# An encoder layer on one core: a wider V projection, column tiles for memory attention, and new homes in on-chip memory

## The chip, the cores and the metric

The kernel runs on one core of a Trainium2 chip. Its time is device microseconds from the start of the program to its end. A core has five engines that run their own instruction streams in order and wait for each other by semaphores: TensorE (PE in the profile, with its weight loads as PEld), VectorE (DVE), ScalarE (ACT), GpSimd (POOL) and SyncE (SP), which here issues most of the transfers. Matrix products read both operands from SBUF (the on-chip memory, 128 partitions) and accumulate in PSUM, eight banks of 2 KB a partition.

## What is computed

One layer of a streaming encoder, all in float32, for 2048 new positions of one prompt and 8 streams ("sample") of 16 positions each. Cut to what matters here:

```python
def encoder_layer(x, past_k, past_v, ..., mk, mv, ...):
    h = rmsnorm(x, g_mix_pre)
    y, new_k, new_v, new_conv = parallel_mixer(h, ...)
    x = x + rmsnorm(y, g_mix_post)
    h = rmsnorm(x, g_mem_pre)
    x = x + rmsnorm(memory_attention(h, mk, mv, w_mq, w_mo), g_mem_post)
    h = rmsnorm(x, g_ffn_pre)
    f = (jax.nn.silu(h @ w_gate) * (h @ w_up)) @ w_down
    return x + rmsnorm(f, g_ffn_post), ...

def memory_attention(h, mk, mv, w_mq, w_mo):          # 4 heads of 256, 256 memory tokens
    q = (h @ w_mq).reshape(B, T, MEM_HEADS, MEM_HEAD_DIM)
    s = jnp.einsum("bthd,bmhd->bhtm", q, mk) * (MEM_HEAD_DIM ** -0.5)
    p = jax.nn.softmax(s, axis=-1)
    o = jnp.einsum("bhtm,bmhd->bthd", p, mv).reshape(B, T, D_MODEL)
    return o @ w_mo
```

The mixer projects h (1024 wide) to q, k, v (512 each) and to the value and gate of a gated unit. Attention has 8 heads of 64 over the own chunk of 64 positions and the 8 chunks before it, with a bias for each head that depends on the clipped distance of query and key. The gated unit goes through a causal convolution of width 31, a layer norm and a swish. Attention and convolution results side by side go through one output projection. The sample streams have memory keys and values of their own, given as input.

## The kernel before, in words

Activations are cut into 17 token tiles of 128 rows: 16 of the prompt and one, `S_TILE`, that holds the 8 sample streams of 16 rows. Nearly every product is made in three passes (`mm3`, L287; `mm3h`, L293): both operands are split into a rounded part "h" (type float32r) and the remainder "l", and high x high, high x low and low x high are summed. So each operand needs a copy on ScalarE (the rounded part) and a subtraction on VectorE or GpSimd (the remainder); for weights both are in `wload` (L275: transfer, L282 copy, L284 subtraction).

The order of stages is memory keys and values of the prompt (`phase_mem`), projections (`phase_proj`), attention, output projection (`mixout`), cross attention of the prompt (`phase_cross`), then the feed-forward stages `gate_up` and `down`. The program is written in one order; a planner with a simulated timeline then sets each engine's instruction order, and may draw an instruction forward when its operands and its place in memory are free. Places are chosen by hand: `Region.lay` and `Region.at` give each name a home in KB of a partition in the areas `sbF`, `sbR`, `fa`, `fb` and the flexible ones, with so many buffers in turn. Two names may share a home, and then the later one waits until the earlier one has been read.

*Projections.* Three groups of two subs of up to three token tiles. In a group come the gated unit (four column blocks j, value and gate), V, then k and q. The convolutions run in the background: each matmul block calls `tick`, which moves `conv_vector` (VectorE, L522) and `conv_pool` (ScalarE L531, GpSimd L532) on. V is made in two column halves `cg` (L630): each loads two blocks of weights, and for each token tile makes 24 products x 2 halves = 48 matmuls of 256 columns. The weight slots "wh" and "wl" have four buffers each, PSUM tile "mm" four. `bias_tables` (L251) spreads the reversed table of the bias over 128 rows in DRAM, [8, 128, 640], early on; attention reads one head of it at a time (L820, L880).

*Attention* (L732) walks through 128 units (head, token tile) and writes its result to `attT` (L873), 32 KB a partition at the start of `sbF`, ordered by head pair, then position. In the background run the sample streams' own attention (`sample`, L756), whose products use column tiles (`tile_position`, L775), and the last convolution norms (`late_norms`). `selectors`, `weigh` and `out_weights` make ready what the output projection needs.

*Output projection* (`mixout`, L963). Order: `S_TILE`, then 0 to 15. `prep` (L980) divides the attention result by the softmax sums: four matmuls of 128 columns (L989) spread the 16 rows of reciprocals (8 heads, rounded part and remainder) over 128 partitions, VectorE multiplies (L991), and the result is split (L997, L998). A token tile then has 48 matmuls of 512 columns (L297). At four points in it `ahead` is moved on, and from the third token tile so is a filler: `due += RATE` at each point, and as many filler steps as are due.

*The filler* is `cross_sample` (L1048), the memory attention of the sample tile. Its steps: query projection (8 steps of 6 matmuls), then 16 jobs (8 streams x 2 halves) for scores, softmax, 16 jobs for values, output projection (8 steps). A job loads 512 KB of memory keys or values (L1070), splits them (L1064, L1065) and makes eight matmuls of 256 columns (L1155, L1192). So that a stream's 16 queries meet only its own keys, they are put in a zeroed tile of 128 columns (`pad`, `blank`, `places` on GpSimd), in two places, and `gather` adds the two halves of the PSUM rows that belong together. Between stages `transposed` turns 128 x 128 blocks (L1080). What is left of the filler after the last token tile runs then.

*Cross attention* (`phase_cross`, L1207) of 16 token tiles begins with `norm(0)` (L1235: load, norm, L324 transposes, split to "sh"/"sl"), eight operands `f1` (L1226: load, L1231 copy, L1232 subtraction) and `scores`.

## Time and profile before

| | us |
|---|---|
| median of 3 runs | 2936.83 (2933.97 to 2940.01) |
| profiled execution, its time | 2935.2 |
| profiled execution, its span | 2933.3 |
| projections, all groups | about 107 to 612 |
| attention | about 612 to 869 |
| output projection with the filler | about 843 to 1119 |
| cross attention | about 1113 to 1515 |

The span is what lies between the first and the last instruction of the program. Stages overlap, so their edges are those of the first and the last matmul of each. In a row of the timeline the first number is the start in microseconds from the span's start, the second the length; "x8" is a run of eight like instructions shown as one, and a bracket gives the engine's idle time before it and what ended it. A group row ends with its count, busy time, mean length in ns and idle time before.

### The profile page before, as it was taken

What the parts mean: (1) busy time and instruction counts of PE and PEld (TensorE: products, weight loads), DVE (VectorE), ACT (ScalarE), POOL (GpSimd) and SP (SyncE); (2) the same over time, 40 slices, a digit from 0 to 9 for tenths busy, and PEclk for the clock granted to TensorE, in tenths of its full rate; (3) what the DMA queues carried; (4) which work ended last, traced back from release to release, by engine and by line L of the source; (5) the groups of instructions that cost most, each with busy time, mean ns of one, the idle gap of its engine ahead of it and who ended that gap; (6) DMA issues with size and microseconds to landing.
All of it is one profiled execution on the core that took longest, in us unless ns stands there. A gap on an engine that the chain in (4) does not pass through costs nothing.

```text
span 2933.3 us, 45550 instructions
## 1 busy us (share of the span) xinstructions
PE 2880.1 (98%) x16688; PEld 2638.1 (90%) x16688; DVE 2130.4 (73%) x3082; ACT 1338.5 (46%) x2631; POOL 1416.6 (48%) x1334
## 2 busy tenths in 40 slices
PE   9999999999999999999999999999999999999998
PEld 8999999988878887888879999999999999888786
DVE  7687895889985666344559888788888997555656
ACT  4435365678873444232344333433344444333433
POOL 1268495731123443154557565465556775424413
PEclk9999999999999999999999999999999999999999
DMA  8645253666635664232354333544344436656664
GB/s 290 245 130 190 94 162 112 218 220 212 224 115 171 220 220 154 69 129 96 129 201 172 116 134 115 200 159 155 141 140 152 145 142 228 224 171 226 225 217 147
DMA packets 201458, 499.53 MB, mean 170 GB/s; under 512 B 19801, under 2 KB 91361, under 8 KB 192394
## 3 DMA queue, kind: packets, MB, share of 16 engines
q1 hardware_dynamic: 186306, 427.01, 43.3%
q0 software_dynamic: 14928, 69.61, 6.4%
q8 instruction: 131, 2.15, 0.3%
q14 instruction: 93, 0.76, 0.1%
HBM read 365.45 MB, written 141.81 MB: 173 GB/s over the span
## 4 chain that ended last, share of the span: by engine, by line
PE 41%; DMA 4%; DVE 3%; POOL 2%; issue 1%; ACT 0%; DVEq 0%; POOLq 0%; SPq 0%; ACTq 0%
PE psb L291 13%; PE psb L290 13%; PE psb L289 13%; DMA sbf<-in_w_down_dram 2%; PE psb L297 1%; POOL sbf L1519 1%; DMA sbf<-x 1%; PE psb L1374 1%; DMA sbf<-hn 1%; DVE sbr L1589 0%; DVE sbr L1397 0%; DMA sbf<-in_w_gate_dram 0%; POOL sbf L347 0%; DVE sbx L1397 0%; DVE sbr L1523 0%
## 5 line engine op out<-in xcount | busy, mean ns | idle before, releaser
L289 PE MATMUL psb<-sbr 128*128 128x384 f32 (+3 forms) x2808 | 940.8, 336 | 4.8 <-DVE sbx L656 1.7
L290 PE MATMUL psb<-sbr 128*128 128x384 f32 (+3 forms) x2356 | 804.2, 341 | 0.5 <-DVE sbr L339 0.3
L291 PE MATMUL psb<-sbr 128*128 128x512 f32 (+3 forms) x1848 | 633.8, 344 | 4.2 <-DVE sbr L1589 4.0
L289 PEld LDWEIGHTS psb<-sbr 128*128 128x128 f32 x2808 | 529.7, 189 | 35.3 <-ACT sbr L1588 2.2
L291 PE MATMUL psb<-sbr,sbx 128*128 128x384 f32 (+2 forms) x1484 | 475.3, 321 | 0.0
L290 PEld LDWEIGHTS psb<-sbr 128*128 128x128 f32 x2356 | 444.4, 189 | 27.5 <-DVE sbr L339 1.0
L291 PEld LDWEIGHTS psb<-sbr 128*128 128x128 f32 x1848 | 348.4, 189 | 34.9 <-DVE sbr L1589 7.8
L297 PE MATMUL psb<-sbr 128*128 128x512 f32 x1200 | 292.5, 394 | 2.6 <-ACT sbr L1267 1.1
L1397 DVE TENSOR_TENSOR sbr<-sbf,sbr 128x512 fp32r<-128x512 f32 x258 | 262.7, 1021 | 39.7 <-ACT sbr L1396 38.9
L1396 ACT CAST sbr<-sbf 128x512 fp32r<-128x512 f32 x258 | 159.3, 620 | 280.2 <-PE psb L290 229.1
L291 PEld LDWEIGHTS psb<-sbr,sbx 128*128 128x128 f32 x1484 | 279.7, 189 | 0.1
L522 DVE SCALAR_TENSOR_TENSOR psb<-sbf,psb 128x768 f32<-128x768 f32 (+1 forms) x290 | 264.3, 911 | 6.2
L297 PEld LDWEIGHTS psb<-sbr 128*128 128x128 f32 x1200 | 222.1, 189 | 49.3 <-ACT sbr L1267 1.3
L1589 DVE TENSOR_TENSOR sbr<-sbf,sbr 128x384 fp32r<-128x384 f32 (+2 forms) x242 | 166.4, 711 | 95.3 <-ACT sbr L1588 94.1
L284 POOL TENSOR_TENSOR sbx<-sbf,sbr 128x1024 fp32r<-128x1024 f32 (+1 forms) x62 | 154.1, 2488 | 81.3 <-ACT sbr L282 70.2
L1588 ACT CAST sbr<-sbf 128x384 fp32r<-128x384 f32 (+2 forms) x242 | 112.5, 483 | 170.5 <-PE psb L290 153.9
L1519 POOL TENSOR_TENSOR sbf<-sbf 128x512 f32<-128x512 f32 x77 | 106.4, 1385 | 168.1 <-DMA sbf<-in_w_down_dram 166.2
L532 POOL TENSOR_TENSOR flexb<-flexb,flexb 128x128 f32<-128x128 f32 (+1 forms) x180 | 168.6, 937 | 26.2 <-ACT flexb L531 17.3
L289 PE MATMUL psb<-sbr,sbx 128*128 128x384 f32 (+1 forms) x524 | 170.6, 327 | 2.3 <-ACT sbx L1396 1.6
L1396 ACT CAST sbx<-sbf 128x512 fp32r<-128x512 f32 x153 | 94.7, 620 | 162.7 <-PE psb L290 142.8
L1397 DVE TENSOR_TENSOR sbx<-sbf,sbx 128x512 fp32r<-128x512 f32 x153 | 153.6, 1005 | 16.1 <-ACT sbx L1396 15.8
L1391 POOL TENSOR_TENSOR sbf<-sbf 128x512 f32<-128x512 f32 x66 | 97.9, 1484 | 107.4 <-DVE sbr L1397 50.7
(335 smaller groups left out, 6080.0 us busy)
## 6 DMA issues: line engine op xcount, KB each, us to landing
af<-flexb SPq DMA_DIRECT2D x33, 1344.0 KB, 5.9
sbf<-in_w_down_dram SPq DMA_DIRECT2D x154, 256.0 KB, 3.8
sbf<-in_w_gate_dram SPq DMA_DIRECT2D x66, 512.0 KB, 3.4
sbf<-in_w_up_dram SPq DMA_DIRECT2D x66, 512.0 KB, 3.4
sbf<-af SPq DMA_DIRECT2D x85, 384.0 KB, 4.1
sbf<-x SPq DMA_DIRECT2D x49, 512.0 KB, 3.7
sbf<-in_w_in_dram SPq DMA_DIRECT2D x48, 512.0 KB, 4.0
sbr<-ks POOLq DMA_DIRECT2D x16, 1024.0 KB, 8.4
```

What stands on the lines that cost most here:

```text
L284: self.lo_engine.tensor_tensor(lo[:, c], wf[:, c], hi[:, c].bitcast(F32), ALU.subtract)
L289: nc.tensor.matmul(ps, lh, rh, start=start, stop=False, **kw)
L290: nc.tensor.matmul(ps, lh, rl, start=False, stop=False, **kw)
L291: nc.tensor.matmul(ps, ll, rh, start=False, stop=stop, **kw)
L297: nc.tensor.matmul(y[o], l, r[:, o * 512:(o + 1) * 512], start=start and x == 0, stop=stop and x == 2)
L522: nc.vector.scalar_tensor_tensor(acc if w < CW - 1 else o, src(w), cwt[:, j, w:w + 1], acc, ALU.mult, ALU.add)
L532: nc.gpsimd.tensor_tensor(o, o, v, ALU.add)
L1396: nc.scalar.copy(hs[j][:, :], src[j])
L1397: nc.vector.tensor_tensor(ls[j][:, :], src[j], hs[j][:, :].bitcast(F32), ALU.subtract)
L1519: nc.gpsimd.tensor_tensor(acc[:, :], acc[:, :], q[:, :], ALU.add if s > 0 else ALU.subtract)
L1588: nc.scalar.copy(ch[:, m], a[:, x, m])
L1589: nc.vector.tensor_tensor(cl[:, m], a[:, x, m], ch[:, m].bitcast(F32), ALU.subtract)
```

## The change

In the order of the program:

- The bias table comes as an input of shape [8, 128, 640]; `bias_tables` is gone.
- V: four weight blocks `w_v[kq]`, each with 512 columns for two of the eight row blocks. A token tile has 24 matmuls of 512 columns; the two column halves are then read from one PSUM tile, in the same copies and stores as before. `tick` is called twice for each token tile.
- Late norms' homes move from 8 to 22 KB of `sbF`.
- `attT` is [P, 16, 4, P]: position tile first, then head pair.
- The selector: `by_column` writes on GpSimd the reciprocals of each head pair to their own 128 columns of a zero-padded tile `rj`, and one matmul of 512 columns takes the place of four. `by_column` is called a quarter of a token tile ahead of `prep`, and `weigh` a quarter later than before.
- Memory attention of the sample tile: `heads` makes four matmuls of 32 columns for a job, one for each head, at column tiles 0, 32, 64 and 96, with unsplit float32 operands (queries and probabilities as `sT`, keys and values straight from their load). A PSUM tile then has 32 rows for each head (16 of the stream, 16 that are not used) and 256 columns for each stream, so the probabilities and the result have 16 blocks to transpose each in place of 8. The softmax is made for four streams at a time, its last product on GpSimd. Padding and gathering are gone.
- `RATE` is 1.3 in place of 1.0.
- `phase_cross`: other homes for "sh", "sl", the operands `f1` and part of `f2`.

```diff
-RATE = 1.0
+RATE = 1.3
...
-                   .lay(sbF, 8, ("thx", 2, 1), ("zx", 2, 2), ("xnx", 2, 2))
+                   .lay(sbF, 22, ("thx", 2, 1), ("zx", 2, 2), ("xnx", 2, 2))
...
-            for cg in range(2):
-                wv = [self.wload(A["w_v"][cg, kh]) for kh in range(2)]
...
+            wv = [self.wload(A["w_v"][kq]) for kq in range(4)]
+            for hsub, sub in zip(hs, subs):
+                hh, hl, _, _ = hsub
+                for i, t in enumerate(sub):
+                    ps = self.t(ps_mm, [P, 512], F32, "mm")
+                    tc_ = slice(i * P, (i + 1) * P)
+                    for k in range(KC):
+                        wh, wl = wv[k // 2]
+                        c = slice((k % 2) * 512, (k % 2 + 1) * 512)
+                        self.mm3(ps[:, :], hh[:, k, tc_], hl[:, k, tc_], wh[:, c], wl[:, c], k == 0, k == KC - 1)
+                    tick()
+                    tick()
...
-        toep = self.toep
+        toep = A["toep"]
...
+    def by_column(self, t):
+
+        R = 2 * H
+        rt = self.rts.pop(t)
+        self.nc.gpsimd.tensor_tensor(self.rj[:R], rt[:, :].bitcast(F32).unsqueeze(1).to_broadcast([R, 4, P]),
+                                     self.own[:, :].unsqueeze(2).to_broadcast([R, 4, P]), ALU.mult)
...
-                for j in range(4):
-                    nc.tensor.matmul(pt[:, j * P:(j + 1) * P], self.expand[:, j, :], rt[:, :], start=True, stop=True)
+                nc.tensor.matmul(pt[:, :], self.spread[:, :, :].rearrange("p o d -> p (o d)"),
+                                 self.rj[:, :, :].rearrange("p j q -> p (j q)"), start=True, stop=True)
...
             if 0 < i < len(order) - 1:
+                self.by_column(order[i + 1])
+                yield
                 prep(order[i + 1])
...
+        def heads(out, s, x, left, right):
+
+            for h_ in range(MH):
+                nc.tensor.matmul(out[32 * h_:32 * h_ + 32, s % 4, :], left(h_), right[:, h_ * NM:(h_ + 1) * NM],
+                                 start=s % 2 == 0 and x == 0, stop=x == 1, tile_position=(0, 32 * h_),
+                                 skip_group_check=True)
...
+        ahead = Ahead([lambda s=s, x=x: load(A["cache_mem_kT"][s, x]) for s, x in jobs])
         yield
+        for s, x in jobs:
+            kx = next(ahead)
+            if x == 0 and s % 4 == 0:
+                sc = self.t(ps_so, [P, 4, NM], F32, "so")
+            heads(sc, s, x, lambda h_: qT[:, 2 * h_ + x, s * DEC_S:(s + 2) * DEC_S], kx)
             yield
+            if x == 1 and s % 4 == 3:
+                g = slice(s - 3, s + 1)
+                nc.vector.tensor_reduce(nmx[:, g], sc[:, :, :], axis=AX.X, op=ALU.max, negate=True)
+                for v in range(s - 3, s + 1):
+                    nc.scalar.activation(z[:, v, :], sc[:, v % 4, :], AF.Exp, bias=nmx[:, v:v + 1],
+                                         accum_out=sm[:, v:v + 1])
+                nc.vector.reciprocal(ri[:, g], sm[:, g])
+                for v in range(s - 3, s + 1):
+                    nc.gpsimd.tensor_scalar(z[:, v, :], z[:, v, :], ri[:, v:v + 1], None, ALU.mult)
...
-                .at("sh", 4, (sbR, [44, 40, 24])).at("sl", 4, (sbR, [52, 48, 28]))
+                .at("sh", 4, (sbR, [96, 44, 24])).at("sl", 4, (sbR, [100, 52, 28]))
...
-        for k, o in enumerate((56, 64, 80, 0, 8, 16, 72, 88)):
+        for k, o in enumerate((64, 80, 88, 0, 8, 16, 72, 56)):
...
-        spots = [(sbR, o) for o in (32, 36, 96, 100, 104)] + [(fr, 4 * i) for i in range(11)]
+        spots = [(sbR, o) for o in (32, 36, 40, 48, 104)] + [(fr, 4 * i) for i in range(11)]
```

More of the change, by code (lines that the diff above doesn't have):

```diff
@@ L1198, in cross_sample @@
-        oT = []
-        yield from transposed(col(of), oT)
+        qT = self.t(pool, [P, KC, P + DEC_S], F32, "sT", 1)
+        nc.gpsimd.memset(qT[:, :, P:], 0.0)
+        for k0 in range(0, KC, 4):
+            nc.scalar.copy(qT[:, k0:k0 + 4, :P], turn(col(q), k0)[:, :, :])
+            yield
+        z = self.t(pool, [P, DEC_B, NM], F32, "sh", 1)
+        nmx, sm, ri = [self.t(pool, [P, DEC_B], F32, x, 1) for x in ("nmx", "sm", "ri")]
+        ahead = Ahead([lambda s=s, x=x: load(A["cache_mem_kT"][s, x]) for s, x in jobs])
@@ new lines, in cross_sample @@
+        yield
+        pT = self.t(pool, [P, 2 * DEC_B, P], F32, "sT", 1)
+        for k0 in range(0, 2 * DEC_B, 4):
+            nc.scalar.copy(pT[:, k0:k0 + 4, :], turn(by_pair(z), k0)[:, :, :])
+            yield
+        of = self.t(pool, [P, DEC_B, NM], F32, "sh", 1)
+        ahead = Ahead([lambda s=s, b=b: load(A["cache_mem_v"][s, b * P:(b + 1) * P, :]) for s, b in jobs])
+        yield
+        for s, b in jobs:
+            vx = next(ahead)
+            if b == 0 and s % 4 == 0:
+                o = self.t(ps_so, [P, 4, NM], F32, "so")
+            heads(o, s, b, lambda h_: pT[:, 2 * s + b, 32 * h_:32 * h_ + 32], vx)
+            if b == 1 and s % 2 == 1:
+                nc.scalar.copy(of[:, s - 1:s + 1, :], o[:, s % 4 - 1:s % 4 + 1, :])
+            yield
@@ L1200, in cross_sample, with token @@
+        def token(k):
+            s, x = k // 2, k % 2
+            return (lambda t: t[:, :, :].rearrange("p (h x) n -> p x h n", x=2)[:, x, :, s * DEC_S:(s + 1) * DEC_S],
+                    lambda pt: pt[:, k % 4, :].rearrange("p (h n) -> p h n", n=32)[:, :, :DEC_S])
+        oT = yield from turned(by_pair(of), [token(k) for k in range(2 * DEC_B)])
         gpost = self.gain(pool, "g_mem_post", "sgain")
@@ L1650, in layout @@
     wv = i["w_in"][0][:, 1024:1536]
[L1651 removed]
+    o["w_v"] = wv.reshape(4, 2, P, 512).transpose(0, 2, 1, 3).reshape(4, P, D)
     o["w_out"] = i["w_out"].reshape(KC, P, D)
```

227 lines of the change are left out of this document (67 added, 160 removed).

## The prediction

> **What bounds the kernel now.** I read the head of the page first, then the busy time by stage. The columns of the second fence are the stretch, its length, the busy time of TensorE, its weight loads, VectorE, ScalarE and GpSimd with their instruction counts, the granted clock, the DMA share and GB/s.
>
> ```profile
> span 2933.3 us, 45550 instructions
> ...
> PE 2880.1 (98%) x16688; PEld 2638.1 (90%) x16688; DVE 2130.4 (73%) x3082; ACT 1338.5 (46%) x2631; POOL 1416.6 (48%) x1334
> ```
>
> ```profile
> 52.00:118.00 66.00, 65.51 (x436) 60.68 (x436) 50.10 (x77) 33.33 (x46) 15.51 (x14) 1.00 0.89 312
> 359.30:394.10 34.80, 34.80 (x293) 34.80 (x292) 31.15 (x40) 21.10 (x31) 31.79 (x18) 1.00 0.46 140
> 913.00:992.00 79.00, 79.00 (x400) 65.13 (x399) 48.03 (x60) 32.34 (x55) 30.16 (x50) 1.00 0.60 205
> 1066.00:1112.00 46.00, 46.00 (x228) 38.61 (x228) 28.75 (x26) 21.05 (x36) 19.02 (x28) 1.00 0.67 237
> 1119.00:1150.00 31.00, 26.06 (x114) 20.89 (x112) 20.62 (x19) 13.01 (x23) 13.45 (x8) 0.94 0.57 190
> ```
>
> TensorE is busy for 98% of the span, and for all of the V stage of the second group (359 to 394 us), of the key part of the sample rows' memory attention (913 to 992) and of the stretch before the stage ends (1066 to 1112). So in these stages a microsecond of matmul taken out is a microsecond off the end, and work taken from VectorE or ScalarE alone is worth nothing. The exception is 1119 to 1150, the hand-over from the output projection to cross attention, where TensorE stands still for 5 of 31 us at a mean clock of 0.94.
>
> **The price of a matmul by its width.** Matmuls overlap, so I take distances between starts, not durations (columns: start, length, engine, line, operation, tiles, shape, count).
>
> ```profile
> 359.33 0.28 PE L289 MATMUL psb<-sbr 128*128 128x256 f32 x1
> ...
> 393.87 1.04 PE L336 MATMUL psb<-ident,sbf 128*128 128x128 f32 x8
> ```
>
> ```profile
> 979.69 5.87 PE L297 MATMUL psb<-sbr 128*128 128x512 f32 x25
> 985.40 1.11 PE L1155 MATMUL psb<-sbr,flexb 128*128 128x256 f32 x8
> 986.35 1.12 PE L1155 MATMUL psb<-flexb 128*128 128x256 f32 x8
> ...
> 990.44 0.66 PE L989 MATMUL psb<-sbr 16*128 16x128 f32 x4
> 991.03 0.39 PE L1155 MATMUL psb<-sbr,flexb 128*128 128x256 f32 x1
> ```
>
> Between the two rows of the first fence lie the 288 V matmuls of six token tiles (48 each): 34.54/288 = 0.120 us for 256 columns. In the second, 25 matmuls of 512 columns take 5.71 us, 0.228 each; a job of memory attention (eight of 256 columns) takes 0.95; the four selector matmuls of a token tile take 0.59.
>
> **V at 512 columns.** A token tile has 48 matmuls of 256 columns and gets 24 of 512: 48 x 0.120 - 24 x 0.228 = 0.29 us, and 17 tiles save 4.9. The copies and stores behind it stay the same instructions.
>
> Its price is the weight buffers. All four 1024-column blocks are now needed by every token tile, so they fill the four "wh"/"wl" slots; before, two were in use while the next two were made ready. A block needs a copy on ScalarE and a subtraction on GpSimd:
>
> ```profile
> 359.39 1.05 ACT L282 CAST sbr<-sbf 128x1024 fp32r<-128x1024 f32 x1 [2.72 <-POOL sbx L284]
> ...
> 360.52 2.41 POOL L284 TENSOR_TENSOR sbx<-sbf,sbr 128x1024 fp32r<-128x1024 f32 x1 [1.76 <-ACT sbr L282]
> ```
>
> ```profile
> 393.67 1.84 POOL L532 TENSOR_TENSOR flexb<-flexb,flexb 128x768 f32<-128x768 f32 x1
> 395.46 4.78 POOL L284 TENSOR_TENSOR sbx<-sbf,sbr 128x1024 fp32r<-128x1024 f32 x2
> ```
>
> From the start of the copy to the end of the subtraction is 3.5 us, and a convolution step of 1.84 us can lie ahead of it on GpSimd, which is busy for 31.8 of 34.8 us here. At the start of V the third block waits for the slot of the last gate block, and its first use comes 12 x 0.228 = 2.7 us later: late by 0.8 us, or 2.6 behind a convolution step. At the end, the first key block waits for the first V slot, which comes free 18 x 0.228 = 4.1 us before the last V matmul: late by 0 to 1.3. Other token tiles' first halves and the next group's transposes can fill such holes. Six edges, three groups with two each: I take 0.7 us an edge, 4 us in all; the bounds are 0 and 2 us an edge, 12.
>
> **The selector.** Four matmuls of 128 columns become one of 512 over zero-padded 128 rows: 0.59 - 0.23 = 0.36 us, over 16 tiles 5.8. In front of it stands a new GpSimd product of 512 columns. Its nearest row:
>
> ```profile
> L1391 POOL TENSOR_TENSOR sbf<-sbf 128x512 f32<-128x512 f32 x66 | 97.9, 1484 | 107.4 <-DVE sbr L1397 50.7 <-DVE sbx L1397 34.6 <-DVE flexb L1397 10.4
> ```
>
> 1.5 us on an engine that is busy for 30 of 79 us in 913 to 992; a quarter of a token tile (3.7 us, below) lies between its call and the matmul, and the selector's consumer is needed half a tile later still. Without that cover it costs 16 x 1.5 = 24 us; I take 0.
>
> **Memory attention in column tiles.** A job's eight full-array matmuls become four of 32 columns, one for each head, side by side, with unsplit f32 operands. The nearest row is the attention of the sample rows, which works so already with 272 columns (eight records: each of the four runs as two passes):
>
> ```profile
> 681.74 0.38 PE L854 MATMUL psb<-ident,flexb 128*128 128x128 f32 x2
> 682.05 0.67 PE L775 MATMUL psb<-sbf,flexb 128*32 128x272 f32 x8
> 682.65 0.39 PE L836 MATMUL psb<-sbr 128*128 128x256 f32 x1
> ```
>
> ```profile
> 1092.29 1.03 PE L1080 MATMUL psb<-ident,flexb 128*128 128x128 f32 x8
> ```
>
> The group takes 0.60 us to the next matmul. A transpose takes (1.03 - 0.27)/7 = 0.11 us, so after the two of the first row the group could have begun at 681.96; it began 0.09 us later. That makes 0.69, for 256 columns some 0.66, against 0.95: 32 jobs save 9.3 us. The bounds are 8.3 (0.69) and 15 (0.48, the streaming alone without the changes of form). The probabilities and the result now need 16 transposes each in place of 8: 16 x 0.11 = 1.8 us more. Net 7.5, bounds 6.5 and 13.
>
> [...]
>
> With the splits go 32 copies of 1.05 us on ScalarE, 32 subtractions on VectorE and all of the padding on GpSimd: nothing, since TensorE is full there. New waits: TensorE now waits for the transfer itself, and the softmax of four streams sits between two groups of jobs on one PSUM tile.
>
> ```profile
> 1141.02 1.23 DVE L1249 TENSOR_REDUCE sbf<-psb 128x4 f32<-128x1024 f32 x1 [5.40 <-PE psb L297]
> 1144.24 0.18 DVE L1256 RECIPROCAL sbf<-sbf 128x4 f32<-128x4 f32 x1 [2.00 <-ACT sbf L1253]
> ```
>
> That chain took 3.2 us in cross attention. A call comes every 3.7 us (a quarter of the 15.0 us token tile worked out below), with output-projection matmuls between; I take 0, bound 3, behind which those matmuls would queue.
>
> **Bias table, token-tile order, early homes.** The table was built at 186 us and first read at 530, so its removal is worth 0; the attention result in the other order costs the same instructions, 0.
>
> What these homes, and the quicker filler, change is the hand-over. The filler had 64 steps and 60 calls at one a call, so the last output-weight matmuls ran after the last token tile; now it has 68 steps and 60 x 1.3 = 78, and ends nearly two tiles early. Cross attention's first tiles no longer lie under the whole attention result, nor its first operands under the last output weights.
>
> ```profile
> 1112.92 1.03 PE L324 MATMUL psb<-ident,sbf 128*128 128x128 f32 x8
> ...
> 1114.77 1.21 PE L297 MATMUL psb<-sbr,sbx 128*128 128x512 f32 x4 [0.35 <-DVE sbr L1065]
> ...
> 1118.12 1.19 PE L297 MATMUL psb<-flexb,sbx 128*128 128x512 f32 x4 [0.74 <-DVE flexb L1065]
> ...
> 1122.56 1.93 PE L324 MATMUL psb<-ident,sbf 128*128 128x128 f32 x8 [3.25 <-DVE sbr L326]
> ...
> 1132.26 3.03 PE L297 MATMUL psb<-sbr 128*128 128x512 f32 x12 [0.59 <-POOL sbr L1232]
> ```
>
> The idle times are 0.35 + 0.74 + 3.25 + 0.59 = 4.9 us. After the longest, eight transposes took 1.93 us against 1.03: the clock had fallen, about 1.9 us with the matmuls behind them. Of 6.8 us I take 5; bounds 0 and 7. Late next is the first probabilities' copy at 1149 us, which no part touches.
>
> **The sum** against the profiled execution's 2935.2 us (span 2933.3, 1.9 around it): -4.9 + 4 - 5.8 - 7.5 - 5 = -19.2, so 2916 us. The runs shown have a median of 2936.8, 1.6 above the profiled one; I leave that inside the range. With all bounds at their best the sum is -32 (2903), at their worst -2 (2933).
>
> **Rivals.** *The weight slots eat it:* each edge of the V stage stands for 4 us (copy, subtraction and a convolution step in a row, nothing to fill); six edges cost 24 instead of 4: 2936, no change. For it: GpSimd is 91% busy there. Against: the holes have work to fill them, and a first half of a token tile is 2.7 us long.
>
> *The transfers bound the filler (slower):* a token tile takes 48 x 0.228 + 5.2 x 0.66 and 0.6 for the rest, 15.0 us, and moves 5.2 x 0.52 MB of cache and 1.3 MB of its own rows, 4.0 MB: 268 GB/s. If these queues gave only the 205 of 913 to 992, a tile would take 19.6 us, and the 32/5.2 = 6.2 tiles of the caches 29 us more: 2945. It decides below 4.0 MB/(15.0 + 19.2/6.2) = 221 GB/s. For it: TensorE now waits for the landing. Against: the same kind of transfer ran at 312 GB/s in 52 to 118, and the queue has landings of
>
> ```profile
> DMA to landing us min/median/max: 3.2/4.2/6.7
> ```
>
> against two calls, 7.4 us, of lead.
>
> *The hand-over stays:* the filler ends early but cross attention's loads are still late on VectorE, 2921; the change then does not do what its homes say. *Column tiles don't run side by side:* four in turn, 4 x 0.48, would add 32 x 0.97 = 31 us: 2947. The rows speak against it, eight records in 0.67 us.
>
> **How the numbers follow.** The forecast with its bounds has 0.67, the hand-over that stays 0.15, the weight slots 0.08, the transfers 0.06, column tiles in turn 0.04 (with any other slower order). Within 0.2% (6 us, about what a measurement here can tell from no change) lie most of the weight-slot case. Faster 0.85, same 0.06, slower 0.09. The range is 2901 to 2933: the bounds of the sum, with 2 us more below since the runs shown lie up to 3 us under their median.
>
> **What would show it.** Right: some 440 fewer TensorE records (V 408, selector 48, plus 16 transposes); L1155 and L1192's successors as groups of eight 32-column records, 0.6 us to the next; TensorE busy about 18 us less; no gap over 1 us before cross attention's first transposes and a clock of 1.00 there. Wrong: TensorE idle on GpSimd's weight subtraction at the V edges; TensorE waiting for DMA of the memory caches; a 3 us gap still at the hand-over.

## The result, and the profile after

The changed kernel takes 2933.84 us (median of 12 runs, 2930.3 to 2939.61) against 2937.35 for the kernel before on the same chips (12 runs): a ratio of 0.9988, with a 95% interval of 0.9978 to 0.9998. So 3.5 us are gained where 19.2 were forecast, and the time lies 0.8 us above the range. The profiled execution took 2939.42 us, near the upper end of its runs, so stages are compared below, not spans.

The lines of the changed kernel are shifted: the three-pass matmuls of the output projection are L279 (before L297), the selector L979 (L989), memory-attention jobs L1095 (L1155, L1192), their transposes L1057 (L1080), the post-norm of a token tile L1031 to L1037 (L1036 to L1042), that of the sample tile L328 to L330 (L346 to L348), cross attention's norm L303, split L307/L308 and transposes L306 (L321, L325/L326, L324), its operands L1188, L1191, L1192 (L1228, L1231, L1232), weight splits L264/L266 (L282/L284), the filler's weight splits L1075/L1076 (L1064/L1065).

The head of the page and the busy time by stage (stretch, length, busy time with instruction counts of TensorE, weight loads, VectorE, ScalarE and GpSimd, granted clock, DMA share, GB/s):

```profile
span 2937.6 us, 44541 instructions
...
PE 2873.1 (98%) x16248; PEld 2594.9 (88%) x16248; DVE 2072.0 (71%) x3053; ACT 1306.7 (44%) x2623; POOL 1413.3 (48%) x1298
```

```profile
913.00:992.00 79.00, 79.00 (x426) 55.46 (x425) 29.02 (x47) 21.39 (x57) 29.00 (x34) 1.00 0.67 234
992.00:1066.00 74.00, 74.00 (x400) 50.24 (x399) 27.84 (x55) 21.72 (x63) 30.21 (x36) 1.00 0.68 233
1066.00:1105.00 39.00, 39.00 (x177) 31.90 (x175) 20.05 (x18) 17.48 (x32) 17.72 (x18) 1.00 0.49 158
1105.00:1119.00 14.00, 6.73 (x19) 5.25 (x19) 7.29 (x6) 4.22 (x5) 11.39 (x10) 0.63 0.32 111
1119.00:1150.00 31.00, 29.31 (x141) 24.06 (x140) 16.70 (x21) 13.35 (x27) 7.94 (x7) 1.00 0.53 175
```

There are 16688 - 16248 = 440 fewer matmul records, as worked out. TensorE's busy time fell by 7.0 us, not 18; apart from the end of the program the changed kernel ran 30.7 us at half clock and the one before 10.2, which lengthens its matmuls (384 columns in 0.32 us at 551.50 us, in 0.18 at 549.04 at full clock) by up to (30.7 - 10.2)/2 = 10 us. TensorE is full through the filler (913 to 1105), with 233 GB/s and more while the caches come in (913 to 1066), so the transfers don't bound it. But from 1105 to 1119 it is busy for 6.7 of 14 us at a clock of 0.63. The timeline there, of all engines (start, length, engine, line, operation, tiles, idle time before and its releaser):

```profile
1095.79 0.63 POOL L1037 DMA_DIRECT2D x<-flexb  x1
...
1103.50 1.28 DVE L328 SCALAR_TENSOR_TENSOR flexb<-psb,flexb 128x1024 f32<-128x1024 f32 x1 [7.21 <-issue]
...
1104.86 3.25 POOL L329 TENSOR_TENSOR flexb<-flexb 128x1024 f32<-128x1024 f32 x1 [7.84 <-DVE flexb L328]
...
1108.44 0.63 POOL L330 DMA_DIRECT2D x<-flexb  x1
...
1111.51 1.41 DVE L1035 SCALAR_TENSOR_TENSOR flexb<-psb,flexb,sbf 128x512 f32<-128x512 f32 x2 [5.60 <-DMA x<-flexb]
...
1112.32 8.44 PE L279 MATMUL psb<-sbr 128*128 128x512 f32 x24 [7.27 <-DVE flexb L1035]
```

Read it from below. TensorE waits 7.27 us with the last column half of the last token tile, since its PSUM buffer is still to be read by the post-norm of the token tile before it (L1035). That post-norm waits 5.60 us for a store: the sample tile's post-norm (L328, add L329, store L330) has just written the one home "po", which both post-norms use with a single buffer, and the home is free only when its store has landed. The sample tile's post-norm had itself been held up by that home: the store of an earlier token tile (L1037, issued at 1095.79) landed at 1103.42, and L328 began at 1103.50, although the profile puts its 7.21 us of idling down to issue. In the kernel before the filler ended behind the last token tile (its post-norm at 1133.2 us, the last token tile's at 1112.8), so the two never met. From 1107.8 us the clock is at half for 10.24 us, of which the last 5.8 fall on matmuls: 7.3 + 5.8/2 = 10.2 us are lost here.

The end of the program is longer too. At its end each engine's stream has records called DRAIN, and the engines then wait for each other (the last DRAIN of all five begins between 2937.1 and 2937.3 us in the changed kernel). These are GpSimd's in the kernel before, and then GpSimd's and SyncE's in the changed one (count, shortest/median/longest in ns, first and last start in us):

```profile
L1702 POOLq DRAIN  x3: 93/188/1343, 2927.4 to 2932.8; - x3
```

```profile
L1663 POOLq DRAIN  x3: 40/102/9014, 2927.8 to 2937.3; - x3
L1663 SPq DRAIN  x3: 7/7/7, 2932.0 to 2937.1; - x3
```

GpSimd's longest takes 1.34 us before and 9.01 us after, where it ends at 2936.8 us while SyncE has come to its own at 2932.0. From the end of the last matmul to the end of the program there are 8.3 to 8.8 us in the kernel before and its three variants (e3, e6, e12 below), and 12.7 to 13.0 us in the changed kernel and its 15 variants: some 4 us that the forecast has no term for. V, the selector, memory attention, the pace and the shared home are not the cause, since each of them was changed back or moved in some variant without changing this. The bias table as an input, the order of the attention result and the other homes remain, and no run tells them apart.

Where the time of each profiled execution went, by the first matmul of attention's scores, of the output projection, and of the transposes of cross attention's first probabilities (us; ratios of all runs to the kernel before, with their 95% intervals):

| kernel | to attention | attention | output projection to probabilities | ratio of times |
|---|---|---|---|---|
| before | 611.9 | 230.7 | 304.3 | 1 |
| after | 608.7 | 232.7 | 301.9 | 0.9988 (0.9978 to 0.9998) |
| after, own home | 608.1 | 233.2 | 293.8 | 0.9953 (0.9941 to 0.9966) |
| own home, product on VectorE | 609.6 | 233.0 | 289.8 | 0.9936 (0.9924 to 0.9949) |
| own home, old selector | 607.9 | 230.9 | 294.1 | 0.9961 (0.9947 to 0.9974) |
| own home, old memory attention | 608.8 | 234.9 | 293.4 | 0.9951 (0.9937 to 0.9965) |
| the same, product on VectorE | 607.8 | 231.4 | 295.2 | 0.9960 (0.9946 to 0.9973) |
| after, V at 256 columns | 611.7 | 232.2 | 300.8 | 0.9991 (0.9982 to 1.0) |
| before, new selector | 613.5 | 231.0 | 297.6 | 0.9972 (0.9962 to 0.9981) |

The stages are those of one execution each. What follows them, to the last matmul, took between 1774 and 1785 us in these and the other executions, though no experiment edits it; so a stage's microsecond or two need not show in the time.

### The profile page after: what moved, and what is told of

It reads as the page before. It is cut to its first block, busy times and chain, and to the rows that moved or that the text cites. A ratio compares the mean times of both kernels' runs of the same rounds, so it can differ in the third digit from the quotient of the medians.

```text
span 2937.6 us, 44541 instructions
## 1 busy us (share of the span) xinstructions
PE 2873.1 (98%) x16248; PEld 2594.9 (88%) x16248; DVE 2072.0 (71%) x3053; ACT 1306.7 (44%) x2623; POOL 1413.3 (48%) x1298
## 4 chain that ended last, share of the span: by engine, by line
PE 41%; DMA 4%; POOL 3%; DVE 3%; issue 2%; ACT 0%; SPq 0%; DVEq 0%; POOLq 0%; ACTq 0%
PE psb L273 13%; PE psb L272 13%; PE psb L271 13%; DMA sbf<-in_w_down_dram 2%; PE psb L279 1%; POOL sbf L1479 1%; DMA sbf<-x 1%; PE psb L1334 1%; DMA sbf<-in_w_gate_dram 0%; DVE sbr L1549 0%; DMA sbf<-hn 0%; DVE sbr L1357 0%; POOL sbf L329 0%; DVE sbx L1357 0%; DMA hn<-sbf 0%
## 5 line engine op out<-in xcount | busy, mean ns | idle before, releaser
L271 PE MATMUL psb<-sbr 128*128 128x384 f32 (+3 forms) x2672 | 916.5, 345 | 4.5 <-ACT sbr L1548 1.7
L272 PE MATMUL psb<-sbr 128*128 128x384 f32 (+3 forms) x2356 | 805.2, 342 | 0.5 <-DVE sbr L321 0.3
L273 PE MATMUL psb<-sbr 128*128 128x512 f32 (+2 forms) x1712 | 610.2, 358 | 3.7 <-DVE sbr L1549 3.6
L271 PEld LDWEIGHTS psb<-sbr 128*128 128x128 f32 x2672 | 503.8, 189 | 40.0 <-ACT sbr L1548 3.5
L272 PEld LDWEIGHTS psb<-sbr 128*128 128x128 f32 x2356 | 445.3, 189 | 27.4 <-DVE sbr L321 1.0
L273 PEld LDWEIGHTS psb<-sbr 128*128 128x128 f32 x1712 | 322.0, 188 | 39.7 <-DVE sbr L1549 7.5
L273 PEld LDWEIGHTS psb<-sbr,sbx 128*128 128x128 f32 x1484 | 280.2, 189 | 1.9 <-POOL sbx L266 1.8
L1356 ACT CAST sbr<-sbf 128x512 fp32r<-128x512 f32 x258 | 159.1, 620 | 275.7 <-PE psb L272 232.2
L279 PE MATMUL psb<-sbr 128*128 128x512 f32 x984 | 244.2, 397 | 9.7 <-DVE flexb L1035 7.3
L279 PEld LDWEIGHTS psb<-sbr 128*128 128x128 f32 x984 | 184.0, 190 | 55.0 <-DVE flexb L1035 7.5
L266 POOL TENSOR_TENSOR sbx<-sbf,sbr 128x1024 fp32r<-128x1024 f32 (+1 forms) x62 | 151.1, 2440 | 80.4 <-ACT sbr L264 70.5
L279 PE MATMUL psb<-sbr,sbx 128*128 128x512 f32 x750 | 186.7, 396 | 2.7 <-DVE sbx L989 1.8
L1479 POOL TENSOR_TENSOR sbf<-sbf 128x512 f32<-128x512 f32 x77 | 107.0, 1393 | 169.8 <-DMA sbf<-in_w_down_dram 168.1
L279 PEld LDWEIGHTS psb<-sbr,sbx 128*128 128x128 f32 x750 | 139.6, 189 | 37.1 <-issue 3.3
```

The costliest lines, as they stand in the source:

```text
L266: self.lo_engine.tensor_tensor(lo[:, c], wf[:, c], hi[:, c].bitcast(F32), ALU.subtract)
L271: nc.tensor.matmul(ps, lh, rh, start=start, stop=False, **kw)
L272: nc.tensor.matmul(ps, lh, rl, start=False, stop=False, **kw)
L273: nc.tensor.matmul(ps, ll, rh, start=False, stop=stop, **kw)
L279: nc.tensor.matmul(y[o], l, r[:, o * 512:(o + 1) * 512], start=start and x == 0, stop=stop and x == 2)
L1356: nc.scalar.copy(hs[j][:, :], src[j])
```

## The experiments

Each kernel's ratio is to the kernel before on the same chip. Many kernels have five runs, and their intervals reach about 0.0013 (4 us) to either side.

### The shared home, and the filler's pace

"Own home" gives the sample tile's post-norm the place of the queries and probabilities, which are read out by then; e1 instead lets the filler run to the end of the stage again.

```diff
-RATE = 1.3
+RATE = 1.15                                    # e1 alone
...
-    def postnorm(self, pool, y, xt, gbc, dst, dma=None, bufs=2):
+    def postnorm(self, pool, y, xt, gbc, dst, dma=None, bufs=2, tag="po"):
-        o = self.t(pool, [P, D], F32, "po", bufs)
+        o = self.t(pool, [P, D], F32, tag, bufs)
...
-                .lay(ft, 0, ("sT", 8, 1))
+                .lay(ft, 0, ("sT", 8, 1)).at("pos", 4, (ft, [0]))
...
+        self.postnorm(pool, flat(y), xt, gpost, self.x2[S_TILE], bufs=1, tag="pos")
```

> The changed kernel, rate 1.3, with a home of its own for the sample tile's post-norm output in place of the single one that it shares with the output projection's token tiles. Theory A1 (the shared home is the longer part of the gap: the next token tile's post-norm waited 5.6 us for the sample tile's store): the gap at 1105 us falls from 7.3 to 3 to 4.5 us, what ScalarE, GpSimd and VectorE need for one post-norm, and the time falls by 3 to 5 us. Theory A2 (the missing cover alone): a gap over 6 us stays, time within 2 us of the changed kernel.

> The changed kernel with a filler rate of 1.15 in place of 1.3: 60 calls give 69 steps, so the 68 filler steps last to the end of the last token tile. Theory A (the 7.27 us gap at 1105 us of the changed kernel stands because the filler is used up two token tiles early, so nothing covers the wait of a token tile's second PSUM half for the post-norm of the one before): no TensorE gap over 2.5 us between 1050 and 1125 us, no half-clock window there, and a time 6 to 10 us under the changed kernel's, about 2926. Theory B (the gap comes from cross attention's first loads, drawn forward into the in-order streams of ScalarE, VectorE and GpSimd): the gap stays within 2 us of 7.3, time within 3 us of the changed kernel.

The own home gave 2927.49 us, 0.9953. Its timeline at the same place:

```profile
1097.69 1.28 DVE L328 SCALAR_TENSOR_TENSOR flexb<-psb,flexb 128x1024 f32<-128x1024 f32 x1 [0.76 <-POOL flexb L289]
...
1101.75 0.60 POOL L330 DMA_DIRECT2D x<-flexb  x1 [0.30 <-POOL flexb L329]
...
1105.23 1.41 DVE L1035 SCALAR_TENSOR_TENSOR flexb<-psb,flexb,sbf 128x512 f32<-128x512 f32 x2 [1.00 <-POOL flexb L289]
...
1106.04 5.32 PEld L279 LDWEIGHTS psb<-sbr 128*128 128x128 f32 x24 [0.26 <-DVE flexb L1035]
1106.04 5.74 PE L279 MATMUL psb<-sbr 128*128 128x512 f32 x24
```

The sample tile's post-norm still stands between two token tiles, but L1035 no longer waits for its store, and TensorE's weight loads wait 0.26 us and its matmuls for nothing the row shows, in place of 7.27. No half-clock stretch follows, the stage is 8.1 us shorter, and the time some 10 us. That is more than theory A1 expected (a gap of 3 to 4.5 us left, 3 to 5 us gained): L328 begins at 1097.69 and no longer at 1103.50, so the home had cost twice. The home is the cause of the gap.

The slower filler of e1 gave nothing (2940.4 us, 0.9999, interval 0.999 to 1.0008), since another wait takes the place:

```profile
1111.65 1.04 ACT L1191 CAST sbr<-sbf 128x1024 fp32r<-128x1024 f32 x1 [7.02 <-DMA sbf<-f1s]
...
1115.85 1.01 ACT L307 CAST sbx<-psb 128x1024 fp32r<-128x1024 f32 x1
...
1116.91 1.22 PE L279 MATMUL psb<-sbr,sbx 128*128 128x512 f32 x2 [6.15 <-ACT sbx L307]
```

ScalarE waits 7.02 us for a weight of cross attention, and the split of cross attention's first token tile (L307) is queued behind it on the same engine. So the filler must neither end late nor write into the shared home. Three runs asked whether the pace alone matters, two of them with the home free.

> The own-home kernel with the filler at 1.2 steps a call in place of 1.3, the control for the run with the old memory attention. If only the shared home was the matter: 0.9953 as with 1.3. If a filler that ends later delays cross attention's first operands, as at 1.15: idle times of 1 us and more appear between 1100 and 1130 us, and the time is 0.997 to 0.999.

> The kernel before with nothing changed but the filler rate, 1.3 in place of 1.0: its 64 steps are used up after 49 of 60 calls, nearly three token tiles early. Theory A: the same kind of gap opens in the last three token tiles (one or more of 3 to 7 us, waiting for the post-norm's VectorE instruction), and the time is 5 to 12 us above the kernel before. Theory B (early homes and early loads make the gap, not the rate): no such gap, and the time is at or below the kernel before, by up to 5 us, since the filler no longer runs past the last token tile.

> The kernel before with the filler at 1.3 steps a call (which alone gave 1.002) and the sample tile's post-norm in another home than the token tiles'. Theory A1 (the shared home is what a filler pays that ends between two token tiles, in either kernel): faster than 1.002 by the gap before the next token tile's matmuls, 1.5 us, and the half clock that follows: about 1.001. Theory B (the old kernel loses to the faster filler because cross attention's first operands and first tiles are late there, under the output weights and the attention result): no change, 1.002 within 0.0005, with the idle times of 2.7, 1.8 and 2.6 us behind the last token tile still there. Neither expects it below 0.9985: a faster filler with a free home is not by itself the gain.

With the own home, 1.2 in place of 1.3 gave 2933.37 us, 0.9978 (0.9969 to 0.9987), 7 us slower; so the home was not the only matter. The wait is that of e1:

```profile
1102.87 0.32 SPq L1164 DMA_DIRECT2D flexb<-x  x1
...
1103.28 3.91 SPq L1188 DMA_DIRECT2D sbf<-f1s  x2
...
1108.45 1.04 ACT L1191 CAST sbr<-sbf 128x1024 fp32r<-128x1024 f32 x1 [3.28 <-DMA sbf<-f1s]
...
1111.95 1.01 ACT L307 CAST sbx<-psb 128x1024 fp32r<-128x1024 f32 x1
...
1113.01 1.22 PE L279 MATMUL psb<-sbr,sbx 128*128 128x512 f32 x2 [5.78 <-ACT sbx L307]
```

On SyncE's queue (SPq) these weight loads stand behind the filler's last load (L1164, the sample tile's own rows), which the slower filler issues at 1102.87; at 1.3 it went out at 1095.27. The kernel before at 1.3 steps a call is slower than at 1.0: 1.002 (1.0011 to 1.0029), and 1.003 (1.0021 to 1.004) with an own home, still with 2.7 us of waiting for ScalarE's L1231 behind the last token tile. There the shared home (moved to another place than in the own-home kernel) is not what costs; the quicker filler pays only together with the other parts.

### V

e4 puts V back to two halves of 256 columns; e5 is the own home with the late subtraction moved.

```diff
+                    self.lo_engine = nc.vector if last and which == 1 and j == 0 else nc.gpsimd     # e5
                     blk = self.wload(A["w_in"][which * 4 + j])
```

> The changed kernel with V as it was, in two column halves of 256. If V at 512 columns is worth what its matmul distances say (4.9 us) less the waits seen at its edges (1.6 us idle at 550 us and a half-clock window of 3.4 us behind it, some 3.3 us in all): the first attention matmul comes 1.5 us later than in the changed kernel, the gap at 550 us is gone, and the time is 0 to 3 us higher. If the weight slots cost more than the matmuls save: the first attention matmul comes earlier and the time is lower by 1 to 4 us.

> The kernel after with the sample tile's post-norm in a home of its own, and besides: in the third group the weight subtraction of the first key block after V is made on VectorE in place of GpSimd. Theory C (the late subtraction at the end of V is a real loss): the idle 1.6 us before the first key matmul at 550 us goes, and with it the half-clock stretch of 3.4 us (1.7 us of work); 3.3 us less than the kernel with the own home alone, about 0.994 of the time before against 0.9953. Rival (the wait is for the weight slot that the last V matmuls hold, whichever engine subtracts): the idle time stays within 0.4 us of 1.6 and the time stays at 0.9953.

In the table V at 512 columns brings attention forward from 611.7 to 608.7 us; in time it is lost in the scatter (0.9991 against 0.9988). Over all executions with nothing changed at the edge, attention began between 607.2 and 609.6 us with V at 512 (12 kernels) and between 611.7 and 614.0 with V at 256 (5 kernels); the means differ by 4.5 us. Four of these five also build the bias table; the fifth, e4, began 3.4 us behind the mean of the 12. Attention then took 232.7 us in the mean of the 12, against 231.1 in the kernel before and its variants, but V is not what costs there: e4, with V at 256, took 232.2, and e8, with V at 512 and the old selector, 230.9. What does is open. One edge of the six shows, the end of V in the last group, where no next group's work fills the hole:

```profile
549.34 0.28 PE L272 MATMUL psb<-sbr 128*128 128x256 f32 x1
551.21 0.49 PE L273 MATMUL psb<-sbr,sbx 128*128 128x384 f32 x1 [1.59 <-POOL sbx L266]
551.50 0.52 PE L271 MATMUL psb<-sbr 128*128 128x384 f32 x1
```

With the subtraction on VectorE the wait fell to 1.12 us, which neither theory had, and the time did not move: 0.9953 (0.9939 to 0.9967). Attention began 1.7 us earlier than in the own-home kernel (606.4 against 608.1), and with the product on VectorE 0.8 us earlier (e15 against e11, 608.8 against 609.6). So the edge is real, and its repair worth too little for these runs to tell in the time.

### The selector

e8 is the own home with the four matmuls of before and no product; e12 the kernel before with the new selector alone; e11 the own home with the product on VectorE.

```diff
-        self.nc.gpsimd.tensor_tensor(self.rj[:R], ...
+        self.nc.vector.tensor_tensor(self.rj[:R], ...          # e11
```

> The own-home kernel with the selector of the kernel before: four matmuls of 128 columns over 16 rows, no product on GpSimd. Theory E (the trace's price: the selector's share of start-to-start time was 9.4 us in the kernel before and 5.0 after): 3.9 to 4.4 us slower than the own-home kernel, 0.9967 of the time before. Prediction's price 5.8 us: 0.9973. Rival E2 (the wait for the product on GpSimd ahead of the matmul eats what the matmuls save): 0.9953, no change.

> The kernel before with the new selector alone (one matmul of 512 columns over 128 padded rows, the product on GpSimd ahead of it). The prediction's price: 5.8 us less, 0.998. Theory E (matmul starts say 4.4 us less): 0.9985. Theory E2 (start-up of the selector at attention's start and the first token tiles' products at the start of the output projection give it back as idle time and half clock): 1.000 within 0.001, with a half-clock stretch near 612 or 872 us that the kernel before has not.

> The own-home kernel with the selector's product on VectorE in place of GpSimd. Theory G (the product on GpSimd holds up VectorE: its 8-element cast took 1.01 us beside the product and 0.17 without it, and so the second token tile's split is late by 0.9 us at 872): the short casts beside it are back at 0.2 us, the idle time at 870 us falls from 1.76 to about 0.9, the half-clock stretch of 871 goes (3.4 us of work), and the time is 3 us under the own-home kernel, 0.9943. Rival G2 (VectorE's own 0.5 us for the product costs the same): 0.9953, the idle time stays over 1.5 us.

Alone in the kernel before, the selector gave 0.9972 (8.2 us; 6.7 in its stage), so the forecast's 5.8 was about right, and the theory that it is given back (E2) fell, though a half-clock stretch of the kind that it named is there, 3.41 us at 875.65. Taken out of the own-home kernel it cost nothing that can be told (0.9961 against 0.9953; 0.3 us in the stage). That kernel, e8, has none of the own home's two half-clock stretches, 6.83 us each at 612 and 872 us; at most 3.4 us of work each, they can hide the selector's gain. For the second the product explains a part. With it on GpSimd (own home), at the start of the output projection:

```profile
870.31 1.34 POOL L939 TENSOR_TENSOR sbr<-sbr,sbf 16x512 fp32r<-16x512 f32 x1 [3.91 <-ACT sbr L933]
...
870.67 1.01 DVE L926 CAST sbr<-sbf 128x8 fp32r<-128x8 f32 x1
...
871.60 1.28 DVE L989 TENSOR_TENSOR sbx<-flexb,sbx 128x512 fp32r<-128x512 f32 x2
...
872.33 2.08 PE L279 MATMUL psb<-sbr,sbx 128*128 128x512 f32 x4 [1.76 <-DVE sbx L989]
```

and with it on VectorE:

```profile
867.00 0.68 DVE L939 TENSOR_TENSOR sbr<-sbr,sbf 16x512 fp32r<-16x512 f32 x1
...
872.67 0.17 DVE L926 CAST sbr<-sbf 128x8 fp32r<-128x8 f32 x1
872.75 1.29 DVE L989 TENSOR_TENSOR sbx<-flexb,sbx 128x512 fp32r<-128x512 f32 x2
...
873.49 2.93 PE L279 MATMUL psb<-sbr,sbx 128*128 128x512 f32 x6 [0.86 <-DVE sbx L989]
```

A cast of eight columns took 1.01 us beside the product and 0.17 without it, and TensorE's wait for the split of the first token tile behind it (L989) fell from 1.76 to 0.86 us. The half-clock stretch there fell from 6.83 to 3.41 us, the stage from 293.8 to 289.8, and the time to 2919.48 us, 0.9936. The interval overlaps that of the own-home kernel (0.9924 to 0.9949, 0.9941 to 0.9966); a second pair with the same difference, e5 and e15, gives 292.5 and 289.1 us in the stage, 0.9953 and 0.9943. So the gain is likely, and a few microseconds at most. Nor is the product needed for such a wait: the kernel before, which has none, waits 1.74 us there (L998), without a half-clock stretch. The long cast ended with the product, both at 871.7 us; what ties the two is not shown.

### Column tiles

e7 issues each job's matmuls twice (so scores and values come out doubled); e10 issues the two jobs of a stream together, 36 steps at 0.7 a call; e13 has the memory attention of before at 1.2 steps a call, and e16 (1.2) and e17 (1.3) the same with the product on VectorE.

```diff
+            for r in range(2):                                                         # e7
             for h_ in range(MH):
                 nc.tensor.matmul(out[32 * h_:32 * h_ + 32, s % 4, :], ...
...
-            yield                                                                      # e10
+            if x == 1:
+                yield
```

> The own-home kernel with the matmuls of each memory-attention job issued twice (the scores and the values come out doubled). It measures what a job of column tiles costs when no change of tiling lies between. Theory D (a job costs 0.57 us of streaming and what it takes to change form once for each call, 0.09 us): 32 x 0.57 = 18 us more than the own-home kernel, 0.9953 + 0.0062 = 1.0015 of the time before. Rival D2 (two passes of 0.24 us are all that streams, the rest is the change of form): 32 x 0.48 = 15.4 us, 1.0005. Rival D3 (the jobs lie in holes of TensorE): under 5 us, below 0.997.

> The own-home kernel with the sample rows' memory attention of the kernel before (eight full-array matmuls a job, split operands, padding on GpSimd; its key caches in the old layout), the filler at 1.2 a call for its 64 steps so that it ends at about the same call. It prices the column tiles as a whole. Prediction's term: 7.5 us slower than the own-home kernel, 0.9979 of the time before. Theory H (start-to-start sums: jobs 31.4 against 25.1 us, transposes 3.1 against 5.3): 4.1 us slower, 0.9967. Rival H2 (what the column tiles save is given back by TensorE waiting, so undoing them costs nothing): 0.9953.

> The own-home kernel with the selector's product on VectorE and the memory attention of the kernel before, the filler at 1.2 a call. Beside the run with column tiles and the product on VectorE (0.9936, and 0.9943 with the edge) it prices the column tiles where the start of the output projection is quiet. Prediction's term: 7.5 us slower, 0.9962 to 0.9968. Sums of matmul starts: 4 us slower, 0.995 to 0.9957. Rival H2 (worth nothing): 0.994.

> The same at 1.3 a call, the pace of the kernel after. If the pace decides only by where the filler ends (64 steps at 1.2 end at the same call as 68 at 1.3; at 1.3 they end a call or two sooner): within 0.0005 of the run at 1.2. If the meeting of single instructions at the hand-over decides: 0.002 or more apart, with an idle time of 3 us and more between 1100 and 1130 us in one of the two.

> The own-home kernel with the two memory-attention jobs of a stream issued together (36 steps at 0.7 a call), nothing else. Theory F: groups of 16 records of 1.00 us instead of groups of 8 of 0.57, 3.6 us less between the first output matmul and cross attention's first probabilities (290.2 in place of 293.8 us), 0.994 of the time before. Rival F2 (transfers): idle times on DMA of the caches, no better than 0.9953.

TensorE's rows of the changed kernel, and then of e7 (32, 16 records in a run):

```profile
984.38 0.64 PE L1095 MATMUL psb<-sbf,flexb 128*32 128x256 f32 x8
984.95 2.57 PE L279 MATMUL psb<-sbr 128*128 128x512 f32 x10
```

```profile
979.02 1.93 PE L1096 MATMUL psb<-sbf,flexb 128*32 128x256 f32 x32
980.88 0.50 PE L279 MATMUL psb<-sbr 128*128 128x512 f32 x1
981.33 1.07 PE L1096 MATMUL psb<-sbf,flexb 128*32 128x256 f32 x16
982.33 3.93 PE L279 MATMUL psb<-sbr 128*128 128x512 f32 x16
```

To the next matmul, eight records take 0.57 us, 16 take 1.00 and 32 take 1.86: each further job 0.43, and 0.14 once. e7 took 0.9992, 11 us more than the own-home kernel, under both expected prices (18 and 15.4) and nearest to 32 x 0.43 = 13.8. The price of a job called by itself, 0.57 + 0.09 ahead of it, is the 0.66 of the prediction.

What the column tiles are worth as a whole came out in two ways. With the product on GpSimd, undoing them cost nothing (0.9951; 293.4 us in the stage against 293.8). With it on VectorE, undoing them cost 0.9960 - 0.9936, 7 us (at 1.3 a call 0.9956, 6 us); in the stage 295.2 and 296.7 against 289.8, so 5.4 and 6.9 us. In the first pair the kernel with column tiles has the 6.83 us at half clock at 872 us, the other 3.41; that accounts for 1.7 us at most, and the rest of the difference is open. e17 against e16 has the pace for its only difference, 0.0004 apart. The kernel with column tiles is not so even: at 1.4 steps a call (e18, below) it gave 0.9961, no faster than e16, so these 6 to 7 us are shown at 1.3 alone.

Jobs in pairs were no gain but a loss, 0.9991 (0.9981 to 1.0). At 1002 us TensorE waited 1.85 us for a transfer, as the rival had it; most went at the hand-over, where the filler's own last weight splits were late at 0.7 a call and cross attention's behind them:

```profile
1001.72 0.64 PE L1095 MATMUL psb<-sbf,flexb 128*32 128x256 f32 x8 [1.85 <-DMA sbf<-in_cache_mem_kT_dram]
```

```profile
1111.67 0.73 PE L279 MATMUL psb<-sbx 128*128 128x512 f32 x2 [1.67 <-DVE sbx L1076]
1112.24 0.63 PE L279 MATMUL psb<-sbr,sbx 128*128 128x512 f32 x2
1114.76 1.97 PE L306 MATMUL psb<-ident,sbf 128*128 128x128 f32 x8 [1.90 <-DVE sbx L308]
```

Nor did the pairs stay together in the planner's order: the 256 records lie in 27 groups, not 16, and 14 of them have eight. So it doesn't tell what joining two jobs in one group is worth.

### Repairs together

> The own-home kernel with all three undone or mended at once: the third group's first key block subtracted on VectorE, the selector of the kernel before, and the two memory-attention jobs of a stream issued together (one call for two jobs, 36 steps at 0.7 a call). The edge and the old selector alone each gave nothing that can be told from the own-home kernel (0.9953 and 0.9961 against 0.9953). Theory F (a job streams for 0.432 us and a call pays 0.228 us once for the change of form there and back, 37 groups become 16): 3.6 us less in the stage of the output projection, and without the half-clock stretches at 612 and 871 us some 3 more: about 2919 us, 0.993 to 0.994. Rival F2 (TensorE waits for the second job's transfer, since only three load buffers serve pairs): no better than 0.9955, with idle times on DMA of the memory caches.

> The own-home kernel with both small repairs: the selector's product on VectorE and the first key block of the third group subtracted on VectorE. Theory G with the edge: the idle times at 550 and 870 us at about 1.1 and 0.9 us in place of 1.6 and 1.8, and no more than the 0.9936 of the product on VectorE alone. If the 0.9936 was within the scatter of the own-home kernel: 0.995.

> The own-home kernel with column tiles and the product on VectorE, the filler at 1.4 a call. At 1.3 this kernel gave 0.9936, at 1.2 (product on GpSimd) 0.9978. If a filler that ends sooner only takes cover away from nothing: 0.9936 again. If single meetings decide: it falls anywhere up to 0.998, with a new idle time at the hand-over that tells it.

e9 fell with the pairs: 1.0015 (1.0006 to 1.0024); why it lies 7 us above the pairs alone (0.9991) no run shows. e15 (product and edge on VectorE) gave 2923.21 us, 0.9943 (0.993 to 0.9956), not to be told from e11. At 1.4 steps a call e18 gave 0.9961 (0.9948 to 0.9975), with a new wait of 2.44 us at the hand-over, for VectorE's L1192. The fastest of the kernels tried is e11: 2919.48 us, 0.9936.

## Why the prediction was wrong

**The step that failed** is the hand-over, the term of -5 us. The prediction had the filler end "nearly two tiles early" and counted that as a gain with 0 for its worst, since "Late next is the first probabilities' copy at 1149 us, which no part touches". It asked what a late filler had held up, and not what its last steps would meet in their new place. They met the post-norm of a token tile in a home with one buffer: 7.27 us of waiting and half clock behind, about 10 us. With that home free these 10 us come back (0.9953 against 0.9988). Of the four idle times of the kernel before three are then gone, as forecast; the fourth, 0.59 us for GpSimd's L1232, stays as 0.56 us for L1192.

**The end of the program** is not in the sum. It grew by about 4 us, on GpSimd's last drain. The bias table's removal was taken at 0 because the table is built and read early; whether that removal is the cause is open.

**The product on GpSimd, "I take 0":** its cover in time was there, but it stood in VectorE's way, 4.0 and 3.4 us in the stage in two pairs of kernels. The bound of 24 us that the prediction names was for another mechanism, and its worst sum, -2, leaves out even that.

**V:** the matmul term, 4.9 us, is borne out (attention began 3.4 to 4.5 us earlier, edges included). The weight slots were oversized: 4 us for six edges, and one shows, 1.6 us, in the changed kernel with a half-clock stretch behind it.

**The selector:** 5.8 us predicted, 6.7 in its stage when alone. **Column tiles:** 7.5 predicted, 5.4 to 6.9 with the product out of the way; 0.66 a call was right, but the planner's order split some jobs (37 groups in place of 32). In the own-home kernel neither shows, for a reason that is known only in part: half-clock stretches that come and go with other waits. The 0.48 us in the bounds of the column tiles was an estimate, and no run shows a job at that price: in the kernel before 0.25 us lie between the starts of the two passes at 272 columns (682.05 and 682.30 us), so about 0.24 at 256, taken twice; e7 has 0.57 for a job alone and 0.43 for each further one. **Softmax, splits, order of the attention result:** no wait of theirs shows.

**Rivals:** transfers bound nothing (TensorE full at 233 GB/s); column tiles do run side by side (eight records in 0.57 us); the one edge that shows is 1.6 us, and their rival had 24. (Column tiles in turn were also added up wrongly: 4 x 0.48 against the forecast's 0.66 is 32 x 1.26 = 40 us on top of 2916, so 2956 and not 2947.) "The hand-over stays" had the right place but another cause. With home and product mended the change takes 0.9936 (0.9924 to 0.9949), 19 us less. That this is the size of the predicted sum is partly luck: it took two repairs that the prediction didn't foresee, it has the 4 us at the end against it, and in the profiled execution, the slowest of that kernel's five, the stages up to cross attention's first probabilities give 14.5 us.

## What to carry to other kernels

When a background task is made to end sooner or later, list what its last steps share with the main loop: homes with a single buffer, the place in each engine's order, the load queue; then work out which of them now meet. A helper moved to an idle engine is priced by what it holds up on its neighbours too, here an eight-column cast at six times its length. Price parts in a kernel whose other waits are quiet: beside the product on GpSimd a gain of six did not show here. And look past the stages that were edited, since here the end of the program grew as well.

## What was not expected of the hardware

Half-clock stretches came in lengths of 3.41 us (3.41, 6.83, 10.24), and an idle time of 1.6 us was followed by one, but not each time. The same stretch, 549 to 556 us, in the changed kernel (idle 1.59 us):

```profile
549.00:556.00 7.00, 5.41 (x22) 5.21 (x22) 6.66 (x10) 3.30 (x8) 7.00 (x4) 0.76 0.68 212
```

and in the own-home kernel (idle 1.60 us):

```profile
549.00:556.00 7.00, 5.39 (x32) 5.19 (x33) 6.75 (x10) 3.55 (x8) 6.97 (x4) 1.00 0.74 216
```

What sets off a stretch is not shown. The product over 16 rows of 512 columns took 1.03 us on GpSimd and 0.68 on VectorE.
